# gMLP mixer of a streaming encoder: the rows of v by VectorE's 32x32 transposes and a DRAM scratch, in a lane of their own

## The chip, the cores and the metric

The kernel runs on one core of one Trainium2 chip. The metric is the device time of one execution in microseconds (us). The time before is 1324.58 us, the median of three runs (1324.56 to 1324.66).

## What is computed

One inference step of a two-layer encoder over 256 prompt frames and 32 sample frames, all in float32. The part that the change touches is the mixer of the odd layer:

```python
def _mixer_c(h, w_in, ln_g, ln_b, w_s, b_s, w_out):
    u, v = jnp.split(jax.nn.gelu(h @ w_in), 2, axis=-1)
    v = _layernorm(v, ln_g, ln_b)
    ...
    mixed = jnp.einsum('gij,bnjgc->bnigc', ws, vg) + b_s...
    return (u * mixed.reshape(B, T, D_C)) @ w_out, v
```

h has 1024 columns, u and v have 2048 each. The layer norm needs statistics over the 2048 columns of each frame. The einsum mixes frames (positions j to i) inside a window of 128 frames, in 8 groups of 256 columns.

## The kernel before

Activations lie transposed: columns on the 128 partitions, the 288 frames (32 of the sample, then 256 of the prompt) along the free axis. The six blocks of the network (`ffn`, `mixer_ab`, `ffn`, `ffn`, `mixer_c`, `ffn`) read their weights as one stream of chunks of up to 8 x 128 rows by 256 columns. SyncE (SP) fetches a chunk into one of three raw tiles `wraw` (`fetch`, L193). `pieces` then splits it in four pieces of 128x512: ScalarE (ACT) writes the rounded high part `wh` (L220), VectorE (DVE) subtracts for the low part `wl` (L221). A full chunk takes 48 products of 288 columns on TensorE (PE): for each of 8 row blocks and 2 column blocks the three products of `mm` (L260 to L262), the first of which reads `wl`. At the chunk's end `evac` (L309, DVE) takes the sums out of PSUM and multiplies them by the norm factor `rb`.

In the program's text, `next_chunk` finishes the splits of its own chunk, and `tick`, called after every 6 products, steps through the splits of the next one and through the lanes. A `Lane` is a list of generators that are worked off one after another, `rate` steps to a tick. This text order is not yet the engines' order: a scheduler places the instructions of every engine anew when the program is built, and each engine then works off its own list from front to back.

`mixer_c` takes 16 chunks of `c_w_in`: v in chunks v0 to v7 first, then u in u0 to u7, then the output projection (o0 and on), two chunks to each 256 output columns. After each v chunk ACT applies the Gelu: the sample's columns go to `vc` (L1005), the prompt's stay in `v` (L1007). The lane step `tokens` then turns v so that frames lie on the partitions: four TensorE transposes of 128x128 into one PSUM tile (L988), and an ACT copy to `vt` (L989); at odd n a fifth transpose for the sample (L994, L995) and `bn_stats` of both windows on DVE (L997). The same lane (`C_RATE` 0.5 steps a tick) holds `spatial_weights`, `row_sums`, and in the u chunks `statistics`, four `normed` (L1038 normalises `vt` and `vs` in place), `sample_out`, and `spatial(n)` for each u chunk: products of `vt` with the mixing weights (L1063, L1082) into the four PSUM tiles of the pool `misc`, DVE steps (L1086, L1089, L1094, L1095), and `put`, which casts u's part to `hh` (ACT, L329) and `hl` (DVE, L330) for the output projection. The u chunks' Gelu is L1102; their tile `u` has four buffers.

`to_rows` (L163), so far used in `mixer_ab` only, transposes a tile in 32x32 blocks on DVE (L168), writes it to a DRAM tile of the pool `rows` with four SP transfers (L172), and leaves it to the caller to read it back.

Of the kernel before, what the change touches and what calls it, by code (L numbers as in the profile page):

```python
# [14 lines left out]
P = 128  # L15
D = 1024
KD = D // P
TP = 256
TS = 32
# [12 lines left out]
WIN = ((32, 160), (160, 288), (0, 128))  # L32
# [40 lines left out]
class Lane:  # L73


    def __init__(self, rate):
        self.rate, self.credit, self.todo = rate, 0.0, []
# [16 lines left out]
class Net:  # L94
# [4 lines left out]
    def __init__(self, tc, ctx, I, O):  # L99
        self.tc, self.nc, self.I, self.O = tc, tc.nc, I, O  # L100
        e = ctx.enter_context
        self.const = e(tc.tile_pool(name="const", bufs=1))
        self.wraw = e(tc.tile_pool(name="wraw", bufs=3))
        self.wspl = e(tc.tile_pool(name="wspl", bufs=4))
        self.acc = e(tc.tile_pool(name="acc", bufs=2, space=PSUM))
        self.misc = e(tc.tile_pool(name="misc", bufs=4, space=PSUM))
        self.nrm = e(tc.tile_pool(name="nrm", bufs=1))
        self.rows = e(tc.tile_pool(name="rows", bufs=2, space=bass.MemoryType.DRAM))
        self.stream, self.pos = [], 0
        self.raw, self.spl = {}, {}  # L110
        self.uid = 0
        self.ahead = None
        self.lanes = []
        self.lv = None
        self.nlane = Lane(self.NORM_RATE)
# [805 lines left out]
    def mixer_c(self, gnext):  # L921
        nc, I, O = self.nc, self.I, self.O
# [3 lines left out]
        with self.tc.tile_pool(name="c", bufs=1, reuse_waits="tile") as pool:  # L926
            self.hidden(pool, 16)
            T = lambda tag, shape, bufs=None: self.t(pool, shape, tag, bufs=bufs)
            lane = Lane(self.C_RATE)
            self.lanes = [lane]  # L930


            J = N // 2
            vt, vs, vc = T("vt", [P, 2, DC]), T("vs", [P, J, P]), T("vc", [P, J, P])
            st = T("st", [P, 3, 4, 6])
# [30 lines left out]
            def row_sums():  # L966
                wsh, wsl = (self.t(pool, [P, 8, P + TS], n, F32R) for n in ("wsh", "wsl"))
                nc.scalar.copy(out=wsh, in_=wsT)
                yield
                nc.vector.tensor_tensor(out=wsl, in0=wsT, in1=wsh.bitcast(F32), op=ALU.subtract)  # L970
                for _ in range(4):
                    yield
                for a, e in ((0, 3), (3, 6), (6, 8)):
                    pt = self.ps("RS")
                    n = (e - a) * (P + TS)
                    mm(pt[:, :n], lhsT=self.onr, rhs=wsl[:, a:e], start=True, stop=False)
                    mm(pt[:, :n], lhsT=self.onr, rhs=wsh[:, a:e], start=False, stop=True)
                    nc.scalar.copy(out=rs[:, a:e], in_=pt[:, :n].rearrange("p (g i) -> p g i", i=P + TS))
                    yield

            def tokens(n, v):
                yield
                pv = self.ps("vt")
                for w in range(2):
                    for b in range(2):
                        s, e = WIN[w]
                        a = 256 * w + P * b
                        nc.tensor.transpose(pv[:, a:a + P], v[:, b, s:e], self.ident)  # L988
                nc.scalar.copy(out=vt[:, :, n * 256:n * 256 + 256], in_=pv.rearrange("p (w c) -> p w c", w=2))  # L989
                yield  # L990
                if n % 2:
                    j = n // 2
                    pv = self.ps("vs")
                    nc.tensor.transpose(pv[:, :P], vc[:, j], self.ident)  # L994
                    nc.scalar.copy(out=vs[:, j], in_=pv[:, :P])  # L995
                    for w in range(2):
                        nc.vector.bn_stats(st[:, w, j], vt[:, w, (n - 1) * 256:(n + 1) * 256])  # L997
                    yield

            spw = spatial_weights()  # L1000
            next(spw)
            for n in range(N):
                v = self.evac(pool, "v", 2)
                a = 2 * TS * (n % 2)
                nc.scalar.activation(out=vc[:, n // 2, a:a + 2 * TS].rearrange("p (b t) -> p b t", b=2),  # L1005
                                     in_=v[:, :, 0:TS], func=AF.Gelu_apprx_tanh)
                nc.scalar.activation(out=v[:, :, TS:], in_=v[:, :, TS:], func=AF.Gelu_apprx_tanh)  # L1007
                lane.todo.append(tokens(n, v))
                if n == 1:
                    lane.todo.append(spw)  # L1010
                if n == 3:
                    lane.todo.append(row_sums())
# [3 lines left out]

            def statistics():
                mv = state["mv"] = T("mv", [P, 3, 2])

                sp = T("sp", [P, 6])  # L1020
                nc.vector.bn_stats(sp, vs.rearrange("p j c -> p (j c)"))
                for k in range(4):
                    nc.vector.tensor_copy(out=st[0:TS, 2, k], in_=sp[TS * k:TS * k + TS])
                for w in range(3):
                    nc.vector.bn_aggr(mv[:, w], st[:, w])
                for k in range(1, 4):
                    nc.vector.tensor_copy(out=mv[TS * k:TS * k + TS, 2], in_=mv[0:TS, 2])
                ve = T("ve", [P, 3])
                nc.vector.tensor_scalar(out=ve, in0=mv[:, :, 1], scalar1=EPS, scalar2=None, op0=add)
                state["rs"] = self.power(ve, 3)  # L1030
                yield
# [9 lines left out]

            def sample_out():

                gb, bb, y = (T(n, [P, J, P]) for n in ("lng", "lnb", "vo"))
                for to, name in ((gb, "c_ln_g"), (bb, "c_ln_b")):
                    for k in range(4):
                        nc.gpsimd.dma_start(out=to[TS * k:TS * k + TS], in_=I[name][0].rearrange(
                            "(j k c) -> k j c", k=4, c=P)[k].partition_broadcast(TS))
                yield
                nc.vector.tensor_tensor(out=y, in0=vs, in1=gb, op=mul)  # L1050
                nc.vector.tensor_tensor(out=y, in0=y, in1=bb, op=add)
                for k in range(4):
                    nc.sync.dma_start(out=O[8][0, 0].rearrange("s (j k c) -> k s j c", k=4, c=P)[k],
                                      in_=y[TS * k:TS * k + TS])
                yield
# [44 lines left out]
            for n in range(N):  # L1100
                u = self.evac(pool, "u", self.C_LAG + 1)
                nc.scalar.activation(out=u, in_=u, func=AF.Gelu_apprx_tanh)  # L1102
                us[n] = u
                if n == 0:
                    lane.todo.append(statistics())
                    for s in range(4):
                        lane.todo.append(normed(s))
                    out = sample_out()
                    next(out)
                lane.todo.append(spatial(n))  # L1110
                if n == 0:
                    lane.todo.append(out)
# [269 lines left out]
```

## Time and profile before

| what | value |
|---|---|
| median of 3 runs | 1324.58 us |
| the profiled execution: its time, and its span | 1324.58 us, 1322.9 us |
| PE, PEld busy | 1317.1 us (100%), 1310.3 us (99%) |
| DVE, ACT, POOL busy | 887.1 us (67%), 661.7 us (50%), 41.7 us (3%) |
| the chain that ended last, by engine | PE 97%, DVE 2% |
| DMA, all queues | 219.83 MB, mean 166 GB/s |

PE is the matmul side of TensorE and PEld its weight loads, which overlap it. Matmuls are pipelined: a product's own record is longer than the distance to the next one's start. "Idle before" an instruction is the time its engine stood still ahead of it. The mixer of the odd layer lies between about 943 and 1118 us of the span; chunk v1's sums are taken at 954.38 us.

### The profile page before, as it was taken

How to read it: one execution, taken by the hardware profiler on the slowest of the kernel's cores; microseconds unless marked ns; L12 is line 12 of the kernel's file. 1: busy time of each engine (PE TensorE's matmuls, PEld its weight loads, DVE VectorE, ACT ScalarE, POOL GpSimd, SP SyncE). 2: the span in 40 equal slices, each digit the busy share in tenths (PEclk: the TensorE clock that was granted, in tenths of full speed). 3: DMA queues.
4: the chain of work that ended last, by engine and by line, in shares of the span. 5: the costliest groups of instructions: out<-in, count | busy, mean ns of one | idle time of the engine just before them, and what ended most of it. 6: DMA issues, size and time to landing. Idle time of an engine off the chain costs nothing.

```text
span 1322.9 us, 24562 instructions
## 1 busy us (share of the span) xinstructions
PE 1317.1 (100%) x9922; PEld 1310.3 (99%) x9922; DVE 887.1 (67%) x1706; ACT 661.7 (50%) x1355; POOL 41.7 (3%) x70
## 2 busy tenths in 40 slices
PE   9999999999999999999999999999999999999998
PEld 9999999999999999999999999999999999999998
DVE  7666556889898866666655756655567976666653
ACT  7544445464746465544444644444655446444432
POOL 1000000010101000000000000030000000000000
PEclk9999999999999999999999999999999999999999
DMA  9555455565565546555545555576544545555453
GB/s 283 178 176 168 150 175 173 157 182 159 168 170 170 140 134 200 161 178 166 157 153 174 165 179 165 161 183 188 169 152 138 167 147 160 173 166 171 152 152 84
DMA packets 254852, 219.83 MB, mean 166 GB/s; under 512 B 41233, under 2 KB 254018, under 8 KB 254738
## 3 DMA queue, kind: packets, MB, share of 16 engines
q1 hardware_dynamic: 253906, 216.32, 53.5%
q0 software_dynamic: 672, 1.77, 0.7%
q8 instruction: 78, 1.28, 0.4%
q10 hardware_dynamic: 160, 0.17, 0.1%
q14 instruction: 36, 0.29, 0.1%
HBM read 210.89 MB, written 7.34 MB: 165 GB/s over the span
## 4 chain that ended last, share of the span: by engine, by line
PE 97%; DVE 2%; ACT 0%; issue 0%; POOL 0%; DVEq 0%
PE acc L262 30%; PE acc L261 30%; PE acc L260 30%; PE sc L623 1%; DVE wl L221 1%; PE sp L1082 1%; PE S L696 0%; PE zs L833 0%; PE acc L1157 0%; PE sc L651 0%; PE ob L900 0%; PE vt L988 0%; PE acc L280 0%; PE z L845 0%; PE ob L895 0%
## 5 line engine op out<-in xcount | busy, mean ns | idle before, releaser
L220 ACT CAST wh<-wraw 128x512 fp32r<-128x512 f32 x768 | 440.5, 619 | 490.3 <-PE acc L262 370.1
L221 DVE TENSOR_TENSOR wl<-wraw,wh 128x512 fp32r<-128x512 f32 x768 | 507.4, 688 | 253.4 <-ACT wh L220 252.9
L260 PE MATMUL acc<-xh,wl 128*128 128x288 f32 x2096 | 627.2, 299 | 0.0
L261 PE MATMUL acc<-xl,wh 128*128 128x288 f32 x2096 | 619.4, 295 | 0.0
L262 PE MATMUL acc<-xh,wh 128*128 128x288 f32 x2096 | 618.9, 295 | 0.0
L261 PEld LDWEIGHTS acc<-xl,wh 128*128 128x128 f32 x2096 | 394.1, 188 | 0.6
L260 PEld LDWEIGHTS acc<-xh,wl 128*128 128x128 f32 x2096 | 393.9, 188 | 0.4
L262 PEld LDWEIGHTS acc<-xh,wh 128*128 128x128 f32 x2096 | 393.6, 188 | 0.2
L260 PE MATMUL acc<-hh,wl 128*128 128x288 f32 x960 | 284.5, 297 | 0.0
L261 PE MATMUL acc<-hl,wh 128*128 128x288 f32 x960 | 283.4, 295 | 0.0
L262 PE MATMUL acc<-hh,wh 128*128 128x288 f32 x960 | 282.8, 295 | 0.0
L260 PEld LDWEIGHTS acc<-hh,wl 128*128 128x128 f32 x960 | 180.2, 188 | 0.8 <-DVE xT L402 0.2
L261 PEld LDWEIGHTS acc<-hl,wh 128*128 128x128 f32 x960 | 180.3, 188 | 0.1
L262 PEld LDWEIGHTS acc<-hh,wh 128*128 128x128 f32 x960 | 180.3, 188 | 0.0
L309 DVE TENSOR_TENSOR u<-acc,rb 128x576 f32<-128x576 f32 x52 | 39.3, 757 | 48.8 <-PE acc L262 48.8
L309 DVE TENSOR_TENSOR g<-acc,rb 128x576 f32<-128x576 f32 x47 | 35.6, 757 | 47.0 <-PE acc L262 47.0
L329 ACT CAST hh<-u 128x576 fp32r<-128x576 f32 x52 | 35.1, 675 | 58.4 <-DVE u L455 40.3
L330 DVE TENSOR_TENSOR hl<-u,hh 128x576 fp32r<-128x576 f32 x52 | 39.4, 758 | 7.1 <-ACT hh L329 1.3
L336 ACT ACTIVATE xh<-xT,cols 128x288 fp32r<-128x288 f32 x40 | 21.2, 531 | 24.8 <-DVE xT L404 15.4
L455 DVE TENSOR_TENSOR u<-u,g 128x576 f32<-128x576 f32 x44 | 33.1, 752 | 0.0
L453 ACT ACTIVATE g<-g 128x576 f32<-128x576 f32 x44 | 30.0, 682 | 0.1
L404 DVE SCALAR_TENSOR_TENSOR xT<-acc,xT 128x288 f32<-128x288 f32 x32 | 14.5, 455 | 17.0 <-PE acc L262 17.0
(303 smaller groups left out, 759.1 us busy)
## 6 DMA issues: line engine op xcount, KB each, us to landing
wraw<-in_ffn_w_up_dram SPq DMA_DIRECT2D x44, 1024.0 KB, 5.9
wraw<-in_ffn_w_gate_dram SPq DMA_DIRECT2D x43, 1024.0 KB, 5.4
wraw<-in_ffn_w_down_dram SPq DMA_DIRECT2D x32, 1024.0 KB, 5.7
wraw<-in_ab_w_in_dram SPq DMA_DIRECT2D x28, 1024.0 KB, 5.0
wraw<-in_c_w_in_dram SPq DMA_DIRECT2D x16, 1024.0 KB, 5.5
wraw<-in_ffn_w_down_dram SPq DMA_DIRECT2D x16, 768.0 KB, 4.6
wraw<-in_c_w_out_dram SPq DMA_DIRECT2D x8, 1024.0 KB, 5.6
wraw<-in_ab_w_out_dram SPq DMA_DIRECT2D x8, 768.0 KB, 5.2
```

What stands on the lines that cost most here:

```text
L220: self.nc.scalar.copy(out=h[:, x], in_=w[:, a:b])
L221: self.nc.vector.tensor_tensor(out=l[:, x], in0=w[:, a:b], in1=h[:, x].bitcast(F32), op=ALU.subtract)
L260: mm(o, lhsT=l[:, k, c], rhs=hi[:, r], start=st, stop=False)
L261: mm(o, lhsT=h[:, k, c], rhs=lo[:, r], start=False, stop=False)
L262: mm(o, lhsT=h[:, k, c], rhs=hi[:, r], start=False, stop=en)
L309: self.nc.vector.tensor_tensor(out=x, in0=acc[:, :, :NT], in1=self.rb, op=ALU.mult)
L329: nc.scalar.copy(out=hh, in_=h)
L330: nc.vector.tensor_tensor(out=self.hl[:, k:k + 2], in0=h, in1=hh.bitcast(F32), op=ALU.subtract)
L336: nc.scalar.activation(out=self.xh[:, k], in_=x, func=AF.Copy, scale=g)
L404: nc.vector.scalar_tensor_tensor(out=x, in0=acc[b][:, :NT], scalar=scale, in1=x, op0=ALU.mult, op1=ALU.add)
L453: nc.scalar.activation(out=g, in_=g, func=AF.Silu)
L455: nc.vector.tensor_tensor(out=u, in0=u, in1=g, op=ALU.mult)
```

## The change

The rows of v no longer go through TensorE. `tokens` now makes two DVE transposes of 128x256 in 32x32 blocks (L168) into a tile named `lnb` or `vo` by turns, four SP writes to DRAM (L172), and two SP reads into `vt` (L989). These steps stand in a lane `fast` with one step a tick; all else stays in the lane with 0.5. The `bn_stats` of a pair of chunks move out into `means` (L982), which an even n calls for the pair before it, and `statistics` for the last pair. The DRAM pool has six buffers instead of two. The tiles `lng`, `lnb` and `vo` of `sample_out` get a flat shape of the same size. The fifth transpose, of the sample, stays.

```diff
--- before.py
+++ after.py
@@ -105,7 +105,7 @@
         self.acc = e(tc.tile_pool(name="acc", bufs=2, space=PSUM))
         self.misc = e(tc.tile_pool(name="misc", bufs=4, space=PSUM))
         self.nrm = e(tc.tile_pool(name="nrm", bufs=1))
-        self.rows = e(tc.tile_pool(name="rows", bufs=2, space=bass.MemoryType.DRAM))
+        self.rows = e(tc.tile_pool(name="rows", bufs=6, space=bass.MemoryType.DRAM))
         self.stream, self.pos = [], 0
         self.raw, self.spl = {}, {}
         self.uid = 0
@@ -926,8 +926,7 @@
         with self.tc.tile_pool(name="c", bufs=1, reuse_waits="tile") as pool:
             self.hidden(pool, 16)
             T = lambda tag, shape, bufs=None: self.t(pool, shape, tag, bufs=bufs)
-            lane = Lane(self.C_RATE)
-            self.lanes = [lane]
+            fast, lane = self.lanes = [Lane(1.0), Lane(self.C_RATE)]
 
 
             J = N // 2
@@ -978,24 +977,26 @@
                     nc.scalar.copy(out=rs[:, a:e], in_=pt[:, :n].rearrange("p (g i) -> p g i", i=P + TS))
                     yield
 
+            def means(j):
+                for w in range(2):
+                    nc.vector.bn_stats(st[:, w, j], vt[:, w, 512 * j:512 * j + 512])
+
             def tokens(n, v):
-                yield
-                pv = self.ps("vt")
-                for w in range(2):
-                    for b in range(2):
-                        s, e = WIN[w]
-                        a = 256 * w + P * b
-                        nc.tensor.transpose(pv[:, a:a + P], v[:, b, s:e], self.ident)
-                nc.scalar.copy(out=vt[:, :, n * 256:n * 256 + 256], in_=pv.rearrange("p (w c) -> p w c", w=2))
+                y = T(("lnb", "vo")[n % 2], [P, 2 * TP])
+                rows = self.to_rows(y, [(TP * b, v[:, b, TS:]) for b in range(2)])
+                for b in range(2):
+                    c = n * 256 + b * P
+                    nc.sync.dma_start(out=vt[:, :, c:c + P],
+                                      in_=rows[TP * b:TP * b + TP].rearrange("(w t) c -> t w c", t=P))
                 yield
                 if n % 2:
                     j = n // 2
                     pv = self.ps("vs")
                     nc.tensor.transpose(pv[:, :P], vc[:, j], self.ident)
                     nc.scalar.copy(out=vs[:, j], in_=pv[:, :P])
-                    for w in range(2):
-                        nc.vector.bn_stats(st[:, w, j], vt[:, w, (n - 1) * 256:(n + 1) * 256])
-                    yield
+                elif n:
+                    means(n // 2 - 1)
+                yield
 
             spw = spatial_weights()
             next(spw)
@@ -1005,7 +1006,7 @@
                 nc.scalar.activation(out=vc[:, n // 2, a:a + 2 * TS].rearrange("p (b t) -> p b t", b=2),
                                      in_=v[:, :, 0:TS], func=AF.Gelu_apprx_tanh)
                 nc.scalar.activation(out=v[:, :, TS:], in_=v[:, :, TS:], func=AF.Gelu_apprx_tanh)
-                lane.todo.append(tokens(n, v))
+                fast.todo.append(tokens(n, v))
                 if n == 1:
                     lane.todo.append(spw)
                 if n == 3:
@@ -1016,6 +1017,7 @@
 
             def statistics():
                 mv = state["mv"] = T("mv", [P, 3, 2])
+                means(J - 1)
 
                 sp = T("sp", [P, 6])
                 nc.vector.bn_stats(sp, vs.rearrange("p j c -> p (j c)"))
@@ -1041,7 +1043,7 @@
 
             def sample_out():
 
-                gb, bb, y = (T(n, [P, J, P]) for n in ("lng", "lnb", "vo"))
+                gb, bb, y = (T(n, [P, J * P]).rearrange("p (j c) -> p j c", c=P) for n in ("lng", "lnb", "vo"))
                 for to, name in ((gb, "c_ln_g"), (bb, "c_ln_b")):
                     for k in range(4):
                         nc.gpsimd.dma_start(out=to[TS * k:TS * k + TS], in_=I[name][0].rearrange(
```

How the change moves instructions. The number in a name counts the tiles of the program, so the same tile has another number in each version. The weights of chunks v7, u0, u1, u2 are `wraw_11212`, `11291`, `11367`, `11442` before, and `wraw_11230`, `11314`, `11405`, `11485` in the change; u3, u4, u5 are `11564`, `11654`, `11746` there.

DVE, from the last chunks of v to the first of u, before: sums of v6 (`v_11437`), v7 (`v_11514`) and u0 (`u_11598`) among the splits `wl`.

```order
L221 TENSOR_TENSOR wl_11485<-wraw_11291,wh_11484 128x512 x2
L221 TENSOR_TENSOR wl_11528<-wraw_11367,wh_11527 128x512 x2
L309 TENSOR_TENSOR v_11437<-acc_11366,rb_10949 128x576
L221 TENSOR_TENSOR wl_11569<-wraw_11367,wh_11568 128x512 x2
L309 TENSOR_TENSOR v_11514<-acc_11441,rb_10949 128x576
L997 BN_STATS st_10885<-vt_10882 128x6 x2
L221 TENSOR_TENSOR wl_11622<-wraw_11442,wh_11621 128x512 x2
L309 TENSOR_TENSOR u_11598<-acc_11518,rb_10949 128x576
```

The same place in the change: sums of v6 are `v_11480`, of v7 `v_11559`.

```order
L221 TENSOR_TENSOR wl_11457<-wraw_11230,wh_11456 128x512 x2
L309 TENSOR_TENSOR v_11480<-acc_11404,rb_10949 128x576
L168 STREAM_TRANSPOSE vo_11417<-v_11400 128x256 x2
L309 TENSOR_TENSOR v_11559<-acc_11484,rb_10949 128x576
L221 TENSOR_TENSOR wl_11494<-wraw_11314,wh_11493 128x512
L982 BN_STATS st_10885<-vt_10882 128x6 x2
L221 TENSOR_TENSOR wl_11494<-wraw_11314,wh_11493 128x512
L221 TENSOR_TENSOR wl_11536<-wraw_11314,wh_11535 128x512 x2
```

Before, the splits of u0 and u1 stand ahead of the taking of v7's sums. In the change the first split of u0 stands behind it.

ACT at the chunks u0 to u2, before: L1102 is the Gelu of u0 (`u_11598`) and u1 (`u_11703`), L220 casts the weights, here of u2 (`wraw_11442`), u3 (`11519`) and u4 (`11613`).

```order
L1102 ACTIVATE u_11598<-u_11598 128x576
L220 CAST wh_11657<-wraw_11442 128x512
L220 CAST wh_11715<-wraw_11519 128x512
L989 COPY vt_10882<-vt_11645 128x2x256
L220 CAST wh_11715<-wraw_11519 128x512
L995 COPY vs_10883<-vs_11667 128x128
L220 CAST wh_11750<-wraw_11519 128x512 x2
L1102 ACTIVATE u_11703<-u_11703 128x576
L220 CAST wh_11790<-wraw_11613 128x512 x2
```

In the change: L1104 is that Gelu, of u0 (`u_11639`), u1 (`u_11742`) and u2 (`u_11831`).

```order
L1104 ACTIVATE u_11639<-u_11639 128x576
L220 CAST wh_11572<-wraw_11405 128x512 x2
L220 CAST wh_11615<-wraw_11405 128x512 x2
L1104 ACTIVATE u_11742<-u_11742 128x576
L220 CAST wh_11662<-wraw_11485 128x512 x2
L220 CAST wh_11714<-wraw_11485 128x512 x2
L1104 ACTIVATE u_11831<-u_11831 128x576
```

Behind the Gelu of u0 there now stand the casts for u1, behind that of u1 those for u2; before, they were those for u2 and u3, and for u4.

DVE at the first `spatial`, in the change: the queue from the last `x` of `spatial(0)` to the first split of u5 (`wraw_11746`).

```order
L1091 SCALAR_TENSOR_TENSOR x_11804<-sp_11825,cols,z_11828 128x256
L1097 TENSOR_TENSOR u_11639<-xs_11783,u_11639 128x2x32
L1096 TENSOR_TENSOR u_11639<-x_11804,u_11639 128x2x256
L1052 TENSOR_TENSOR vo_11644<-vs_10883,lng_11642 128x512
L1088 SCALAR_TENSOR_TENSOR z_11897<-RS_10887,cols,BS_10888 128x128
L330 TENSOR_TENSOR hl_10881<-u_11639,hh_10880 128x576
L1053 TENSOR_TENSOR vo_11644<-vo_11644,lnb_11643 128x512
L1091 SCALAR_TENSOR_TENSOR x_11893<-sp_11894,cols,z_11897 128x256
L1088 SCALAR_TENSOR_TENSOR z_11917<-RS_10887,cols,BS_10888 128x128
L221 TENSOR_TENSOR wl_11933<-wraw_11746,wh_11932 128x512
```

Before, the same steps stand between splits, here of u4 (`wraw_11613`) and u5 (`wraw_11707`), one or two steps and then a split:

```order
L221 TENSOR_TENSOR wl_11836<-wraw_11613,wh_11835 128x512
L1074 TENSOR_TENSOR xs_11803<-xs_11803,zs_11802 128x128
L221 TENSOR_TENSOR wl_11836<-wraw_11613,wh_11835 128x512
L1089 SCALAR_TENSOR_TENSOR x_11822<-sp_11823,cols,z_11826 128x256
L1095 TENSOR_TENSOR u_11598<-xs_11803,u_11598 128x2x32
L221 TENSOR_TENSOR wl_11882<-wraw_11707,wh_11881 128x512
L1050 TENSOR_TENSOR vo_11603<-vs_10883,lng_11601 128x512
L221 TENSOR_TENSOR wl_11882<-wraw_11707,wh_11881 128x512
```

In the change nine `normed` steps (L1040) and twelve steps of `spatial` and `sample_out` follow each other without a split, after the four splits of u4. On PE they meet these products: the spatial products of groups 0 and 1 stand after 33 of the 48 products of chunk u4, where before they stood 12 products apart from chunk u3 on.

## Rows read from the trace of the kernel before

**Rows 1.** The page: the chain by engine; VectorE's splits, busy us, mean ns | idle before.

```profile
PE 97%; DVE 2%; ACT 0%; issue 0%; POOL 0%; DVEq 0%
...
L221 DVE TENSOR_TENSOR wl<-wraw,wh 128x512 fp32r<-128x512 f32 x768 | 507.4, 688 | 253.4 <-ACT wh L220 252.9
```

**Rows 2.** Windows: stretch, length; PE, PEld, DVE, ACT, POOL busy; PEclk, DMA share, GB/s.

```profile
945.00:1002.00 57.00, 56.98 (x432) 56.63 (x431) 37.31 (x66) 35.35 (x72) 0.00 (x0) 1.00 0.52 165
...
1019.00:1063.00 44.00, 44.00 (x345) 44.00 (x344) 42.71 (x97) 20.91 (x36) 0.00 (x0) 1.00 0.48 150
```

**Rows 3.** The chain, v chunks: start us, length us, what.

```profile
953.28 0.66 PE vt L988 x4
...
957.53 0.44 PE vt L988 x4
```

**Rows 4.** Tile vt: the transposes, duration ns min/median/max, first and last start.

```profile
L988 PE MATMUL vt<-ident,v x32: 270/272/328, 953.3 to 1006.4; 128*128 128x128 f32 x32
```

**Rows 5.** Timeline, PE and DVE at a chunk's end: start us, length us, what.

```profile
36.18 0.30 PE L262 MATMUL acc<-xh,wh 128*128 128x288 f32 x1
36.31 0.29 PE L260 MATMUL acc<-xh,wl 128*128 128x288 f32 x1
...
36.52 0.76 DVE L309 TENSOR_TENSOR u<-acc,rb 128x576 f32<-128x576 f32 x1 [1.20 <-PE acc L262]
```

**Rows 6.** Timeline, DVE and ACT from the sums of v6 to the next splits.

```profile
994.15 0.76 DVE L309 TENSOR_TENSOR v<-acc,rb 128x576 f32<-128x576 f32 x1
...
994.94 0.26 ACT L1005 ACTIVATE vc<-v 128x64 f32<-128x64 f32 x1 [0.20 <-DVE v L309]
...
995.80 1.14 ACT L220 CAST wh<-wraw 128x512 fp32r<-128x512 f32 x2
...
996.45 1.29 DVE L221 TENSOR_TENSOR wl<-wraw,wh 128x512 fp32r<-128x512 f32 x2 [1.55 <-ACT wh L220]
...
998.45 1.28 DVE L997 BATCH_NORM_STATS2 st<-vt 128x6 f32<-128x512 f32 x2
```

**Rows 7.** Timeline, ACT: a u chunk's Gelu and the casts behind it.

```profile
1027.00 0.69 ACT L1102 ACTIVATE u<-u 128x576 f32<-128x576 f32 x1
1027.59 1.12 ACT L220 CAST wh<-wraw 128x512 fp32r<-128x512 f32 x2
```

**Rows 8.** Groups of DVE by form, 940 to 1075 us: busy us, mean ns | idle before.

```profile
L1089 DVE SCALAR_TENSOR_TENSOR x<-sp,cols,z 128x256 f32<-128x256 f32 x16 | 7.6, 479 | 0.5 <-PE sp L1082 0.5
...
L330 DVE TENSOR_TENSOR hl<-u,hh 128x576 fp32r<-128x576 f32 x8 | 6.0, 753 | 1.3 <-ACT hh L329 1.3
L1086 DVE SCALAR_TENSOR_TENSOR z<-RS,cols,BS 128x128 f32<-128x128 f32 x16 | 5.5, 345 | 0.0
L1094 DVE TENSOR_TENSOR u<-x,u 128x512 f32<-128x512 f32 x8 | 5.5, 686 | 0.1
```

**Rows 9.** Timeline, DVE at the normalisation.

```profile
1013.54 0.16 DVE L1029 TENSOR_SCALAR ve<-mv 128x3 f32<-128x3 f32 x1
1014.70 1.00 DVE L1038 TENSOR_SCALAR vt<-vt,mv,pw 128x512 f32<-128x512 f32 x2 [1.00 <-POOL pw L134]
```

**Rows 10.** The chain at the mixer's end.

```profile
1070.32 0.40 PE acc L260
```

**Rows 11.** Line 168: DVE's 32x32 transposes, ns min/median/max.

```profile
L168 DVE STREAM_TRANSPOSE kn<-bv x4: 760/763/765, 268.1 to 451.6; 128x576 f32<-128x576 f32 x4
```

**Rows 12.** SP's timeline at a scratch write; DMA issues: KB each, us to landing.

```profile
242.91 2.05 SPq L172 DMA_DIRECT2D rows<-QK  x4
...
wraw<-in_c_w_in_dram SPq DMA_DIRECT2D x16, 1024.0 KB, 5.5
...
rows<-QK SPq DMA_DIRECT2D x16, 80.0 KB, 2.1
```

**Rows 13.** PE at the span's start (timeline), and spatial products in the chain.

```profile
1.16 3.36 PE L1157 MATMUL acc<-ones 128*128 128x128 f32 x14 [1.16 <-DVE ms L1168]
...
1060.79 1.78 PE sp L1082 x16
```

## The prediction, made before the result was known

> **What bounds the kernel now.** I read the page first: the chain of waits is 97% TensorE [rows 1]. The windows view says the same of the gMLP mixer: in the v chunks TensorE works 56.98 of 57 us, VectorE 37.3 and ScalarE 35.4; in the spatial part VectorE too is nearly full, 42.7 of 44 us [rows 2]. So a product taken from TensorE shortens the kernel by its distance to the next one, and anything that makes TensorE wait lengthens it by the wait. There is no slack in which a wait could vanish. What the reader is to see in the timeline is the reserve that keeps TensorE fed: VectorE stands idle for 1.20 us until the last product of a chunk has passed, takes the sums 0.34 us after that product's start, and TensorE's next product has long started, 0.13 us after it [rows 5]. It could, because the next chunk's weights were split beforehand.
>
> **What is removed.** 32 transposes. Each group of four fills 0.44 us of the chain, and the first one 0.66 because it waits for the Gelu [rows 3]: 7 x 0.44 + 0.66 = 3.7 us gained. A record of such a transpose lasts 272 ns [rows 4], but records overlap, and the distance of 0.11 counts. The Trainium skill, TensorE: Matmul & The Clock Gate, Part 4, gives about 275 ns for a transpose inside a kernel; the trace has that length too. By it the gain would be 32 x 0.275 = 8.8 us and the forecast below 5 us lower; the chain decides for 3.7. ScalarE loses eight copies, in idle time.
>
> **What is added.** 16 VectorE transposes of 256 columns. The nearest row has 763 ns for 576 columns [rows 11], so 0.34 us each by columns, 0.76 at most: 5 to 12 us in a stretch of 57 where VectorE idles for 20 [rows 2]. They cost nothing themselves. The DMAs: per chunk four writes, 2.05 us of SP's time, landing in about 2.1 us, and two reads, behind which the next weight fetch waits in SP's queue [rows 12]. A fetch lands in 5.5 us and is asked for more than a chunk (6.4 us) before its first split; in the new order the splits come later still, so I cost it at nothing. Without that cover a late fetch would cost its lateness.
>
> **What is moved is what counts.** The engines' orders show that the scheduler has laid VectorE's and ScalarE's queues anew. Before, the splits of u0 and u1 stand ahead of the taking of v7's sums. In the change the first split of u0 stands behind it, that of u1 behind u0's, and so on to u4. An engine works off its list from front to back, so VectorE idles through the chunk's products, and TensorE then waits for it. I add up each exposed chain, from the start of a chunk's last product; TensorE would otherwise go on after 0.13 us.
>
> Start of u0: 0.34 until VectorE takes v7's sums [rows 5], 0.67 until its next instruction starts (0.76 less 0.09, by which two splits of 0.69 that fill 1.29 overlap), 0.69 for the split [rows 1, 6], 0.03 for the hand-over to TensorE, taken as that from VectorE to ScalarE (994.15 + 0.76 to 994.94), less 0.13: 1.6 us.
>
> Starts of u1, u2, u3, u4: here ScalarE's queue has the Gelu of the chunk just ended ahead of the casts for the next, so the chain goes through both engines: 0.34, sums 0.76, hand-over 0.03, Gelu to cast 0.59 [rows 7], cast to split 0.65 [rows 6], split 0.69, hand-over 0.03, less 0.13 gives 2.96. The same chain stands in the trace once, hidden: from 994.15 to the end of the first split at 996.45 + 0.69 [rows 6] it takes 2.99, of which 0.16 are the extra Gelu on `vc`; with 0.34, 0.03 and 0.13 that makes 3.07. I take 3.03: four times, 12.1 us.
>
> Second splits: at u0, u2 and u4 a pair of `bn_stats` (1.2 us, [rows 6]) stands between the first and second split, 1.9 us from split to split where the first piece feeds 12 products, 1.6 us: 0.2 to 0.4 each, partly hidden at u0. 0.6 us.
>
> Spatial steps in u4: let T be the start of its first product. Two statistics, the aggregates and three splits bring `ve` to T+2.6; GpSimd's power and the way back take 1.16 [rows 9]; the nine `normed` steps, 0.46 apart, run from T+3.8 to T+8.0, the sample's (third) being done at T+5.25. TensorE wants it after 33 products, at T+4.8: 0.5 waited. The next waiting is for PSUM: the four `misc` tiles hold the first four spatial results, and the eighth group needs the fourth result read. That read is the eleventh step after `normed`: starts 0.2, 0.4, 0.2, 0.4, 0.14, 0.6, 0.6, 0.26, 0.67, 0.6 apart (the means less the overlap [rows 8], 0.6 also for the two steps on the output `vo`, 0.2 and 0.14 for the small ones), so it starts at T+12.0 and ends at T+12.5; TensorE gets there at T+10.0 (spatial pairs at 0.44 [rows 13]). 2.5 waited. The first split of u5 stands two places behind, done at T+13.35, and TensorE is ready at T+12.95: 0.4. Together 3.4 us.
>
> From u5 on VectorE's work for a chunk (4 splits, sums, one `spatial`) is about 6.3 us against 6.4 of products and 0.9 of spatial pairs, so the queue keeps pace. At the end of the mixer TensorE already lost a little before (0.40 instead of 0.13 [rows 10]). In the new order the first split of the second output chunk stands behind the last steps of `spatial(7)`, some 0 to 2.5 us of VectorE's work ahead of it [rows 8]; I take 1.3 us, the middle.
>
> **Sum:** -3.7 + 1.6 + 12.1 + 0.6 + 3.4 + 1.3 = +15.3 us. The profiled execution took 1324.58 us, the same as the median of the runs (its span is 1322.9), so I predict 1340 us. By the bounds (2.9 to 3.2 for each of the four chains, spatial 2 to 5, end 0 to 2.5) the likeliest case runs from 1336 to 1344.
>
> **Rivals.**
>
> 1. The clock falls. TensorE has never been idle this long in the trace, and its granted clock is 1.00 throughout [rows 2]; before its first work, products of 128 columns came 0.24 us apart against 0.11 later [rows 13], the ratio of 1.2 to 2.4 GHz, for about 4.5 us. If each of four waits of 3 us brought that back, each would cost 2.3 us more: 1349 us. For it: waits of 3 us in 9.4. Against it: two thirds of that time is dense work. 10%. The Trainium skill, TensorE: Matmul & The Clock Gate, Part 1, has the array fall back to 1.2 GHz after idling; no run here shows whether 3 us suffice.
>
> 2. The casts are not in the chain: if ScalarE had the next casts done before the Gelu, each of the four starts would cost 1.6 us as at u0, 5.7 less in all: 1334 us. The order speaks against it, since the Gelu stands ahead of the casts. 4%.
>
> 3. The rows of v land late, and `bn_stats` waits for the scratch. From transposes to landed reads I bound it by 0.8 + 2.05 + 2.1 + 0.75 + 5.5, some 11 us [rows 12]; the last pair's statistics stand three chunks behind its transposes, over 20 us. If a read were 4 us over that, TensorE would wait: 1344 us. 3%.
>
> 4. Faster: the gain stays alone. That needs TensorE to have the next chunk's first split at hand at each of the five starts, as it has today [rows 5], so that less than 3.7 us are waited in all; the point from which it decides is one and a quarter exposed chains. 1324.6 - 3.7 = 1320.9 us. The only way is that the queues as executed let a split pass a waiting instruction; the idle 1.20 us on VectorE ahead of each taking of sums [rows 5] speaks against it. 3%.
>
> 5. Only one chain is exposed, for a reason that I don't see: 3.7 lost, 3.7 gained, no change. 2%.
>
> **How the numbers follow.** The likeliest case has what remains, 78%. About 0.2%, 2.7 us, is what a measurement of this kernel tells from no change. Faster by more: rival 4, 0.03. Within: rival 5, 0.02. Slower: all others, 0.95. The range from 1335 to 1346 holds the likeliest case, rival 3 and part of a falling clock (one to three of the four waits), and leaves out a good tenth.
>
> **What would show it.** In the changed kernel's profile TensorE's busy share stays high by its modelled records, but its weight loads should show idle times of about 1.6 us once and 3 us four times, released by `wl` L221, one behind each of the chunks v7, u0, u1, u2 and u3, then 0.5, 2.5 and 0.4 us around the first spatial products; VectorE should idle 4 to 5 us ahead of its L309 there, and ScalarE's Gelu L1104 be followed at once by casts, each followed by a split and TensorE's start. The stretch between the sums of v7 and of u3 should take four times 9.4 us instead of 6.4. The prediction is wrong if TensorE runs through these starts, if a wait for `vt` or for `wraw` from DMA stands ahead of a split, or if the granted clock leaves 1.00.

## The result and the profile after

The changed kernel takes 1347.69 us (median of 4 runs, 1346.91 to 1348.67) against 1324.57 for the kernel before: ratio 1.0175, 95% interval 1.0157 to 1.0192. It is slower, as forecast, but 7.7 us beyond the forecast of 1340 and outside its range of 1335 to 1346. The profiled execution took 1348.28 us, 23.7 more than that of before, with a span of 1346.6 us.

The page, beside [rows 1]: the chain by engine, then two groups (busy us, mean ns | idle before).

```profile
PE 91%; DVE 4%; issue 3%; ACT 1%; POOL 0%; POOLq 0%; DVEq 0%; ACTq 0%
...
L260 PE MATMUL acc<-xh,wl 128*128 128x288 f32 x2096 | 631.0, 301 | 13.3 <-DVE wl L221 13.1
...
L260 PEld LDWEIGHTS acc<-xh,wl 128*128 128x128 f32 x2096 | 397.9, 190 | 14.9 <-issue 14.1
```

TensorE's share of the chain falls from 97 to 91%, and 13.3 us of idle time, 13.1 of them ended by VectorE's split, stand ahead of the first product of a chunk. The windows (columns as in [rows 2]): first the v chunks, then one from each start of u0 to u4 to the next, the last of these up to the wait of the spatial products, then the spatial part:

```profile
945.00:1002.00 57.00, 54.77 (x407) 53.93 (x406) 38.51 (x82) 28.25 (x60) 0.00 (x0) 1.00 0.71 185
993.10:1001.40 8.30, 6.76 (x52) 6.54 (x51) 7.11 (x18) 1.04 (x3) 0.00 (x0) 1.00 0.43 137
1001.40:1012.40 11.00, 8.11 (x50) 7.90 (x50) 3.94 (x7) 2.75 (x5) 2.17 (x4) 0.84 0.96 217
1012.40:1024.60 12.20, 9.31 (x50) 9.10 (x50) 4.44 (x7) 2.75 (x5) 0.00 (x0) 0.72 0.53 170
1024.60:1035.60 11.00, 8.11 (x50) 7.91 (x50) 3.25 (x5) 2.75 (x5) 0.00 (x0) 0.84 0.31 97
1035.60:1049.20 13.60, 10.71 (x74) 10.51 (x73) 11.13 (x26) 6.23 (x12) 1.25 (x1) 0.87 0.24 77
1049.20:1060.20 11.00, 8.99 (x56) 8.57 (x55) 11.00 (x27) 3.96 (x7) 0.00 (x0) 0.84 0.30 78
```

The column before the last two tells what the sum of waits missed: a chunk takes 11.0, 12.2 and 11.0 us instead of the forecast 9.4, and the granted clock in it is 0.72 to 0.84, where it was 1.00 in the stretches of before [rows 2]. One start, that of u2, in the timeline of VectorE and ScalarE:

```profile
1012.83 0.76 DVE L309 TENSOR_TENSOR u<-acc,rb 128x576 f32<-128x576 f32 x1 [5.81 <-PE acc L262]
1013.62 0.68 ACT L1104 ACTIVATE u<-u 128x576 f32<-128x576 f32 x1 [8.25 <-DVE u L309]
1014.21 2.16 ACT L220 CAST wh<-wraw 128x512 fp32r<-128x512 f32 x4
1014.84 0.69 DVE L221 TENSOR_TENSOR wl<-wraw,wh 128x512 fp32r<-128x512 f32 x1 [1.26 <-ACT wh L220]
1015.45 1.28 DVE L982 BATCH_NORM_STATS2 st<-vt 128x6 f32<-128x512 f32 x2
```

and in that of TensorE's weight loads, of which there is one to each product:

```profile
1012.23 0.19 PEld L261 LDWEIGHTS acc<-xl,wh 128*128 128x128 f32 x1
1012.37 0.19 PEld L262 LDWEIGHTS acc<-xh,wh 128*128 128x128 f32 x1
1015.65 0.29 PEld L260 LDWEIGHTS acc<-xh,wl 128*128 128x128 f32 x1 [3.10 <-issue]
1015.82 0.33 PEld L261 LDWEIGHTS acc<-xl,wh 128*128 128x128 f32 x1
1016.06 0.33 PEld L262 LDWEIGHTS acc<-xh,wh 128*128 128x128 f32 x1
```

Here is the forecast chain: sums, Gelu, cast, split, TensorE, 3.28 us from the last product of u1 to the first of u2, and VectorE idle for 5.81 us ahead of the sums. Behind it products start 0.24 us apart instead of 0.13, which is 1.2 instead of 2.4 GHz; 25 of them in this chunk, 13, 15 and 13 behind the starts of u1, u3 and u4, and 14 from 1052.5 on, behind the wait of the spatial products. At 0.107 us more each, the 80 products cost 8.5 us.

The waits add up from the same column of starts. Over all distances above 0.26 us in the mixer, less 0.13 for each, the trace gives 19.86 us, that of before 0.73. So: 19.1 of waits, 8.5 of half clock, less 32 x 0.11 = 3.5 for the transposes: 24.1, where the profiled executions differ by 23.7. I use this account for every run below.

### The profile page after: what moved, and what is told of

Same layout as the page of the kernel before. It is cut to its first block, busy times and chain, and to the rows that moved or that the text cites. A ratio compares the mean times of both kernels' runs of the same rounds, so it can differ in the third digit from the quotient of the medians.

```text
span 1346.6 us, 24619 instructions
## 1 busy us (share of the span) xinstructions
PE 1323.6 (98%) x9890; PEld 1315.0 (98%) x9890; DVE 891.0 (66%) x1722; ACT 656.8 (49%) x1347; POOL 41.9 (3%) x70
## 4 chain that ended last, share of the span: by engine, by line
PE 91%; DVE 4%; issue 3%; ACT 1%; POOL 0%; POOLq 0%; DVEq 0%; ACTq 0%
PE acc L262 28%; PE acc L261 28%; PE acc L260 28%; DVE wl L221 1%; PE sc L623 1%; PE S L696 0%; PE zs L833 0%; ACT wh L220 0%; DVE x L1091 0%; PE acc L1159 0%; PE sc L651 0%; PE ob L900 0%; DVE vt L1040 0%; PE acc L280 0%; PE z L845 0%
## 5 line engine op out<-in xcount | busy, mean ns | idle before, releaser
L220 ACT CAST wh<-wraw 128x512 fp32r<-128x512 f32 x768 | 439.1, 618 | 487.5 <-PE acc L262 367.4
L260 PE MATMUL acc<-xh,wl 128*128 128x288 f32 x2096 | 631.0, 301 | 13.3 <-DVE wl L221 13.1
L260 PEld LDWEIGHTS acc<-xh,wl 128*128 128x128 f32 x2096 | 397.9, 190 | 14.9 <-issue 14.1
L337 DVE SCALAR_TENSOR_TENSOR xl<-xT,cols,xh 128x288 fp32r<-128x288 f32 x40 | 20.6, 514 | 8.5 <-ACT xh L336 8.5
```

What stands on the lines that cost most here:

```text
L220: self.nc.scalar.copy(out=h[:, x], in_=w[:, a:b])
L260: mm(o, lhsT=l[:, k, c], rhs=hi[:, r], start=st, stop=False)
L337: nc.vector.scalar_tensor_tensor(out=self.xl[:, k], in0=x, scalar=g, in1=self.xh[:, k].bitcast(F32), op0=ALU.mult, op1=ALU.subtract)
```

## The experiments

Two questions: what lays the splits behind the sums, and whether the clock's 8.5 us come from TensorE's idleness. "Half-clock products" are those that start 0.24 us behind the one before instead of 0.13, or, for the shorter spatial products and transposes, 0.21 instead of 0.11.

**e1. The writes on GpSimd.**

```diff
-            nc.sync.dma_start(out=to[q], in_=y[TS * q:...
+            (q_ or nc.sync).dma_start(out=to[q], in_=y[TS * q:...
...
-                rows = self.to_rows(y, [...])
+                rows = self.to_rows(y, [...], nc.gpsimd)
```

> The changed kernel with the four scratch writes of a chunk issued by GpSimd; the two reads stay on SP, and nothing else is edited. Theory (the loss comes from where the scheduler puts the splits, and it puts them late because of the writes in SP's queue): in the new order the first split of u0 to u4 stands 5 to 9 places ahead of the taking of the sums of the chunk before, so TensorE does not wait there; the 32 transposes stay gone, the granted clock stays at 1.00: 1324.6 - 3.7 = 1321 us (1319 to 1323). Rival A (the transposes on VectorE and the trip through DRAM cost the time themselves, wherever they are issued): four waits of about 3 us remain at the starts of u1 to u4, 1337 to 1348 us. Rival B (GpSimd's issuing is slow and the rows land late): a wait for vt ahead of bn_stats, 1323 to 1335 us.

Measured: 1326.45 us (11 runs, 1324.10 to 1328.18), ratio 1.0012 [1.0003, 1.0021]. VectorE's order, around the sums of v7 (line, operation, out<-in):

```
L221 TENSOR_TENSOR wl_11573<-wraw_11405,wh_11572 128x512 x2
L309 TENSOR_TENSOR v_11559<-acc_11484,rb_10949 128x576
L221 TENSOR_TENSOR wl_11616<-wraw_11405,wh_11615 128x512 x2
```

These are splits of u1; all four of u0 stand ahead of them again, and 21 of the 23 us are gone with one edit that leaves every transpose on VectorE and every byte of the trip. Rival A falls. The waits at the starts of u0 to u4 are gone altogether; what remains is rival B, at another place. The timeline, VectorE and TensorE's weight loads:

```profile
1016.77 1.29 DVE L982 BATCH_NORM_STATS2 st<-vt 128x6 f32<-128x512 f32 x2 [1.32 <-DMA vt<-rows]
...
1018.30 0.19 PEld L260 LDWEIGHTS acc<-xh,wl 128*128 128x128 f32 x1
1021.12 0.50 PEld L1065 LDWEIGHTS sp<-wsB,vs 128*128 128x128 f32 x2 [2.63 <-issue]
```

The last statistics wait 1.3 us for rows from DRAM, the normalised `vs` is late by so much, and the first spatial product waits 2.7 us; 15 half-clock products follow. So the rows explain half of this wait; the rest is left to the 4.4 us from these statistics to that product. A transpose of `vc` adds 0.8. The runs part by the clock as well: those with a mean of 1.000 took 1324.1 to 1325.3, those with 0.997 1328.0 and 1328.2.

**e2. The order by hand.**

```diff
+            with self.tc.manual_schedule(engines={mybir.EngineType.DVE}):
                 for n in range(N):
                     v = self.evac(pool, "v", 2)
                     ...
```

> The changed kernel with VectorE's instructions of the v chunks kept in the order in which the program writes them; all scratch transfers stay on SP. Theory (the order alone makes the loss): the first splits of u0 to u4 stand 5 to 24 places ahead of the sums, no waits at these starts, clock 1.00: 1321 us (1318 to 1324). Rival (SP is really too slow: with six transfers a chunk in its queue the weights of the next chunk land late, and the scheduler's late places only mirror that): TensorE waits at the starts of u1 to u4 all the same, now for a split that waits for wraw from DMA: 1335 to 1348 us.

Measured: 1329.26 us (5 runs), ratio 1.0039 [1.0026, 1.0051]. Neither was right. With all six transfers of a chunk still on SP the starts of u1 to u4 do not wait, so SP's queue does not make those waits on the chip. But in the program's order VectorE comes to `bn_stats` before the rows are there (timeline in chunk u0; the last two rows show what stands behind it):

```profile
999.00 1.29 DVE L982 BATCH_NORM_STATS2 st<-vt 128x6 f32<-128x512 f32 x2 [4.53 <-DMA vt<-rows]
1000.21 1.88 DVE L221 TENSOR_TENSOR wl<-wraw,wh 128x512 fp32r<-128x512 f32 x3
1000.93 0.19 PEld L260 LDWEIGHTS acc<-xh,wl 128*128 128x128 f32 x1 [1.45 <-DVE wl L221]
```

Three such waits, 9.4 us on VectorE, come through to TensorE as 1.2 to 1.5 us behind the first twelve products of v4, v6 and u0, where the second split is wanted, and the transposes of `vc` in these chunks then wait 1.1 each. The profiled run has no half-clock products; two of the other four show a mean clock of 0.997 and 0.998.

**e3 and e9. Work in the waits.** The dummy products write columns 384 to 511 of a PSUM tile, which nothing reads. As the scheduler places them, the trace of e3 has 8 ahead of u0 and 12 ahead of each of u1 to u4. In e9 the last three counts are 9 instead of 12.

```diff
+        for _ in range(self.fill):
+            self.nc.tensor.matmul(acc[0][:, 384:512], lhsT=self.ones, rhs=self.ones, start=True, stop=True)
         self.mm(acc, ch, (self.xh, self.xl), self.KORD, True, True)
...
+                self.fill = (7, 12, 1, 12, 12, 12, 0, 0)[n]
                 u = self.evac(pool, "u", self.C_LAG + 1)
```

> The changed kernel with dummy products added (ones by ones, into columns of the next chunk's PSUM tile that nobody reads), 8 ahead of u0 and 12 ahead of each of u1 to u4; they sit in TensorE's queue where it waits. VectorE's order is that of the changed kernel. Theory (the 7.7 us beyond the sum of the waits come from the granted clock, which falls because TensorE stands idle in each wait): the distance from the last product of a chunk to the first of the next stays near 3.2 us, the clock stays at 1.00 and the time falls by 6 to 8 us, to 1340 us (1339 to 1342), though work is added. Rival (the clock falls for another reason, or the 7.7 us lie elsewhere): 1346 to 1350 us with a clock below 1.00 as in the changed kernel.

> As e3 with 9 instead of 12 dummy products ahead of u2, u3 and u4. In e3 the dummies at these starts began only 1.27 us after the chunk's last product (they wait for the PSUM tile until VectorE has taken the sums) and 12 of 0.22 us then ran 0.66 past the end of the wait, so that the start took 3.94 us instead of 3.28. Theory: starts of 3.3 us again, the clock still at 1.00 behind them, 3 x 0.66 less than e3: 1340.7 us (1339.5 to 1341.7), 7 us under the changed kernel though it waits as long. Rival (the clock in e3 stayed up because the distances were other ones, not because TensorE worked in them): half clock again behind these starts, 1344 us or more.

Measured: e3 1342.67 us (4 runs), ratio 1.0141 [1.0127, 1.0155]; e9 1342.30 us (4 runs), ratio 1.0134 [1.0119, 1.0150]. Windows of e9, from start to start as above:

```profile
1001.50:1010.90 9.40, 9.28 (x74) 9.09 (x73) 3.94 (x7) 2.75 (x5) 2.17 (x4) 1.00 0.96 221
1010.90:1020.60 9.70, 8.85 (x69) 8.51 (x68) 4.44 (x7) 2.75 (x5) 0.00 (x0) 1.00 0.73 208
1020.60:1030.10 9.50, 8.65 (x68) 8.41 (x68) 3.26 (x5) 2.76 (x5) 0.00 (x0) 1.00 0.46 151
```

VectorE and ScalarE do what they did in the changed kernel, a chunk's first product still starts 3.2 to 3.3 us after the last of the chunk before, and the clock stays at 1.00: 9.4, 9.7 and 9.5 us where it was 11.0, 12.2 and 11.0. That is the prediction's 9.4. So the clock fell there because TensorE stood idle; adding work made the kernel 5.4 us faster. Both runs missed their figure, by 2.7 and 1.6 us. In e3 twelve dummies were too many, and three starts took 3.94 us. In both, TensorE, no longer slowed, is early at the spatial products: in e9 it waits 0.9 us ahead of the first, where the changed kernel has no wait, and again 2.5 at a later one, with 12 half-clock products behind it in the profiled run; two of the four runs show a mean clock of 1.000.

**e4. The trip beside the transposes.** Nobody reads the rows here.

```diff
                 nc.scalar.copy(out=vt[:, :, n * 256:...     (TensorE's transposes stay)
+                y = T(("lnb", "vo")[n % 2], [P, 2 * TP])
+                rows = self.to_rows(y, [...])
+                for b in range(2):
+                    nc.sync.dma_start(out=z[:, :, P * b:P * b + P], in_=rows[...])
```

> The kernel before with tokens(n, v) in the lane of its own and with the scratch trip added beside the TensorE transposes: VectorE transposes each chunk into y, SP writes it to DRAM and reads it back into a tile that nobody uses; vt still comes from TensorE, and bn_stats stand where they stood before. Theory (SP's transfers in the scheduler's plan push the splits behind the sums; neither the removal of the transposes nor the lane does): the first splits of u1 to u4 stand 1, 9, 8 and 6 places behind the sums, TensorE waits 3 us or more at each, the clock falls with it: 1338 to 1352 us, over the 1324.6 of before. Rival (the loss belongs to what the change takes from TensorE or to bn_stats waiting for the rows): within 3 us of 1324.6.

Measured: 1337.05 us (4 runs), ratio 1.0097 [1.0082, 1.0113]. TensorE loses nothing of its work, the statistics wait for no row, and the kernel is 12.5 us slower, of which e5 puts 1.6 down to the lane: the trip alone lays the order anew, and by e1 it is its writes in SP's queue that do it. The time is 1 us under the range, and the theory had the waits too long: TensorE stands 4.0 us at the start of u1, but 1.4 at that of u2 and 0.1 and 0.8 at u3 and u4, with 1.1 and 2.0 ahead of spatial products, and half-clock products follow at u1 alone. The longest of the waits, at the start of u1:

```profile
1004.48 0.19 PEld L262 LDWEIGHTS acc<-xh,wh 128*128 128x128 f32 x1
...
1006.21 1.00 DVE L1043 TENSOR_SCALAR vt<-vt,mv,pw 128x512 f32<-128x512 f32 x2 [1.00 <-POOL pw L134]
1007.12 0.75 DVE L309 TENSOR_TENSOR u<-acc,rb 128x576 f32<-128x576 f32 x1
1007.79 1.88 DVE L221 TENSOR_TENSOR wl<-wraw,wh 128x512 fp32r<-128x512 f32 x3
...
1008.58 0.19 PEld L260 LDWEIGHTS acc<-xh,wl 128*128 128x128 f32 x1 [3.91 <-issue]
```

**e5. The lane alone.**

```diff
-            lane = Lane(self.C_RATE)
-            self.lanes = [lane]
+            fast, lane = self.lanes = [Lane(1.0), Lane(self.C_RATE)]
...
-                lane.todo.append(tokens(n, v))
+                fast.todo.append(tokens(n, v))
```

> The kernel before with tokens(n, v) in the lane of its own and nothing else of the change: TensorE's transposes stay, no trip through DRAM, bn_stats where they stood. Theory (the lane does no harm): every first split stands 4 places or more ahead of the sums, no new waits, 1324.5 us (1323.5 to 1326). Rival (steps that run right behind the Gelu make TensorE wait for v, or push the splits back): 1327 us or more, with waits of PEld ahead of the transposes into vt.

Measured: 1326.15 us (10 runs), ratio 1.0013 [1.0003, 1.0022], between the two figures. The order is harmless, as the theory has it, but the rival's wait is there: TensorE's transposes now stand 0.2 to 0.8 us for the Gelu, eight times, 2.5 us in all (one of them, 0.3, is in before too). The lane is worth little either way.

**e6, e7, e8, e10. Some chunks by rows, the rest by TensorE.** With `HYB` = 6, 4, 6 and 7; e8 keeps all transfers on SP and the old place of the transposes of `vc`.

```diff
+                if n >= HYB:
+                    ...                     (the transposes of before)
                 y = T(("lnb", "vo")[n % 2], [P, 2 * TP])
-                rows = self.to_rows(y, [...])
+                rows = self.to_rows(y, [...], nc.gpsimd)
...
                 if n % 2:
+                    yield
                     j = n // 2
```

> Writes issued by GpSimd as in e1, but only the chunks v0 to v5 go by way of the scratch; v6 and v7 keep TensorE's transposes, so that the statistics no longer wait for the last rows; and the transposes of vc come one step later. Theory (what e1 still lost was the wait of 2.8 us ahead of the first spatial product, the half clock behind it, and the 0.9 us ahead of a transpose of vc): 24 transposes gone, 24 x 0.11 = 2.7 us less than before, none of these waits: 1321.8 us (1321 to 1323.5). Rival (rows from DRAM cost something that no wait shows): 1324 to 1326 us.

> As e6 with v0 to v3 by way of the scratch and v4 to v7 by TensorE's transposes. Theory: 16 transposes gone, 1.8 us less than before: 1322.7 us (1321.8 to 1324), about 0.9 us over e6. Rival: no order between e6, e7 and before.

> The changed kernel with v0 to v5 by way of the scratch, all transfers on SP, and v6 and v7 by TensorE's transposes. In its order the first splits of u0, u1 and u2 stand 2, 1 and 1 places behind the sums, those of u3 on 9 and more ahead. Theory (each exposed start costs its wait and, where it is as long as the four of the changed kernel, about 1.5 us of half clock): -2.7 + 1.8 at u0 + 2 x 3.15 + 2 x 1.5 + 0.5 for a transpose of vc = about +9: 1333.5 us (1330 to 1337). Rival A (SP's six transfers a chunk delay the weights themselves): waits at u3 and u4 too, 1337 us or more. Rival B (the clock needs four waits in a row to fall): 1330 us, clock 1.00.

> As e6 with v0 to v6 by way of the scratch and v7 alone by TensorE's transposes: 28 transposes gone. Theory: 28 x 0.11 = 3.1 us less than before, 1321.6 us (1320.8 to 1323), if the rows of v6, now the last to land, are there when the statistics want them. Rival: they are not, a wait ahead of the first spatial product as in e1, 1323 us or more.

Measured: e6 1322.10 us (11 runs), ratio 0.9983 [0.9974, 0.9992]; e7 1323.27 (11 runs), 0.9993 [0.9985, 1.0002]; e8 1334.47 (4 runs), 1.0074 [1.0060, 1.0088]; e10 1327.47 (8 runs), 1.0025 [1.0015, 1.0036].

e6 is faster than both kernels, by 2.4 us of the 2.7 forecast; e7 lies 1.2 over it, not told from before by its interval, in the order forecast. In e6 TensorE's windows are full again, beside [rows 2]:

```profile
945.00:1002.00 57.00, 57.00 (x428) 56.46 (x427) 43.22 (x88) 34.20 (x71) 19.78 (x32) 1.00 0.82 231
1019.00:1063.00 44.00, 44.00 (x343) 43.89 (x341) 41.51 (x93) 21.28 (x37) 0.00 (x0) 1.00 0.49 150
```

e8 puts the same rows back on SP and loses 12 us: u0, u1 and u2 are exposed, as its order says, and u3 and u4 are not. Windows of e8, one that holds the start of u0, one from the start of u1 to that of u2, one with the start of u2:

```profile
994.30:1005.70 11.40, 8.95 (x56) 8.53 (x55) 7.61 (x18) 3.71 (x8) 0.00 (x0) 0.85 0.53 172
1005.70:1013.90 8.20, 6.66 (x51) 6.45 (x50) 3.16 (x5) 0.68 (x1) 0.00 (x0) 1.00 0.39 125
1013.90:1024.00 10.10, 6.75 (x37) 6.05 (x36) 7.67 (x17) 5.97 (x11) 1.25 (x1) 0.83 0.25 76
```

Rivals A and B both fall: two of three waits, at u0 and u2, brought half clock, and in e1 and e10 one wait alone does. The split of the loss was other than forecast: 2.9 at u0 (a transpose of v7 for its Gelu, then the split), 1.8 at u1, 3.15 at u2, 1.0 ahead of a spatial product.

e10 comes out as its rival has it, by other rows. One chunk more by rows, and the statistics ask for rows that are not there (timeline: VectorE, SP, TensorE's weight loads):

```profile
983.13 0.77 DVE L168 STREAM_TRANSPOSE vo<-v 128x256 f32<-128x256 f32 x2
...
995.86 3.50 SPq L1008 DMA_DIRECT2D vt<-rows  x4
...
1005.90 1.29 DVE L982 BATCH_NORM_STATS2 st<-vt 128x6 f32<-128x512 f32 x2 [4.11 <-DMA vt<-rows]
...
1014.68 0.50 PEld L1085 LDWEIGHTS sp<-wsB,vs 128*128 128x128 f32 x2 [4.47 <-issue]
```

The transposes shown are those of v5: the semaphores that these statistics wait for are those that tell of the landing of v4's and v5's reads, not of v6's, whose statistics at 1008.90 do not wait for DMA. From v5's transposes to the statistics 22.8 us pass. Its reads, the first two of the four shown, are issued behind a weight fetch in SP's queue and have landed at 1005.78; in e6 the same reads have landed at 1001.95. Whether v6's reads, issued just behind them, made the difference is not shown. TensorE then stands 4.5 us ahead of the first spatial product, and 22 half-clock products follow.

**The account.** Microseconds against before, from the profiled executions; waits as above, less before's 0.7 (in e3 and e9 they include the dummies):

| run | waits | half clock | transposes gone | sum | measured |
|---|---|---|---|---|---|
| changed | 19.1 | 80: 8.5 | -3.5 | 24.1 | 23.7 |
| e1 | 3.9 | 15: 1.6 | -3.5 | 2.0 | 1.9 |
| e2 | 8.2 | 0 | -3.5 | 4.7 | 4.4 |
| e3 | 21.9 | 11: 1.2 | -3.5 | 19.6 | 19.5 |
| e4 | 11.7 | 14: 1.5 | 0 | 13.2 | 12.4 |
| e5 | 2.3 | 0 | 0 | 2.3 | 1.3 |
| e6 | 0.3 | 0 | -2.6 | -2.3 | -2.5 |
| e7 | 0.8 | 0 | -1.8 | -1.0 | -1.4 |
| e8 | 10.0 | 23: 2.5 | -2.6 | 9.9 | 10.0 |
| e9 | 20.7 | 12: 1.3 | -3.5 | 18.5 | 18.1 |
| e10 | 4.6 | 22: 2.4 | -3.1 | 3.9 | 3.8 |

Every run closes within 1.0 us, without a fourth term.

## Why the prediction missed

**What bounds the kernel: right.** To 0.4 us, the result is waits and slower products of TensorE, less the transposes.

**What is removed: right.** 0.11 us per transpose holds; e7 to e6, eight transposes more, are 1.2 us, and e6's 24 are 2.4. The transposes' records of 0.27 us, by which 24 would give 6.5, are ruled out.

**What is added: right in the changed kernel.** VectorE's transposes last 0.42 us (inside the bounds of 0.34 and 0.76) and lie in its idle time; the weight fetches land in 5.9 instead of 5.5 us, and no split there waits for one:

```profile
wraw<-in_c_w_in_dram SPq DMA_DIRECT2D x16, 1024.0 KB, 5.9
...
L168 DVE STREAM_TRANSPOSE lnb<-v x8: 398/418/446, 952.7 to 1000.4; 128x256 f32<-128x256 f32 x8
```

**What is moved: right in place, and nearly in price.** Waits of 19.1 us where the terms gave 19.0; that they agree to 0.1 is partly luck, since terms that came out smaller or not at all make up for chains that are 0.1 to 0.2 us longer and for a wait that was not foreseen:

| step | forecast | measured |
|---|---|---|
| start of u0 | 1.6 | 1.8 |
| starts of u1 to u4 | 4 x 3.03 | 4 x 3.15 |
| second splits | 0.6 | 0, in none of the distances |
| spatial steps in u4 | 0.5 + 2.5 + 0.4 | 0 + 2.15 + 0.4 |
| end of the mixer | 1.3 | 1.7 more than before |
| a transpose of `vc` ahead of its Gelu | none | 0.8 |

The 0.5 was hidden, since TensorE at half clock came later to it, and so were the second splits of u2 and u4: in e9, at full clock, the first is 0.9, the others 0.2 and 0.3. At u0 the second split waits in neither. The prediction put the moved splits down to the scheduler; e1, e4 and e8 add the reason, SP's transfers in the scheduler's plan. Why its plan sends splits back for them is not seen in a trace and stays open.

**The step that failed is the clock.** The sum prices every product behind a wait at full pace, that is, the falling clock at nothing; only rival 1 has it, with a chance of 10%, held down by "two thirds of that time is dense work", and the range had room for one to three such falls. The fall came on top of the likeliest case, behind all four waits of 3.28 us and a fifth time behind the spatial wait: 80 products at half clock, 8.5 us, and e3 and e9 show that those behind the starts go away when TensorE works in the waits. The Trainium skill, TensorE: Matmul & The Clock Gate, Part 1, says that the array falls back to 1.2 GHz after idling; the prediction noted that no run showed whether 3 us suffice. Here they did, at all four starts, and so the question bore on the price of the likeliest case, not on a side case. That the rival's 1349 us is only 1.3 over the result is partly luck: it had 2.3 us behind each of four waits, from the slow products at the span's start, and the runs show 1.4, 2.7, 1.6 and 1.4, with 1.5 at the fifth place, which it did not name. (In the trace of before, the slow products at the span's start follow each other in 0.21 us, not 0.24, and go on until 6.4 us, not 4.5.) Take the 8.5 us off the profiled 1348.28, and 1339.8 is left, where 1340 was forecast. That too is partly luck: e9 shows that a kernel with these waits and a full clock takes 1342, since part of what the half clock takes had covered other waits.

**Rival 3 did not occur, but depends on the order.** In the changed kernel no `bn_stats` waits. The prediction bounded the trip by some 11 us; in e2, with all transfers on SP as there, the statistics that wait for rows start 10.7, 12.0 and 10.8 us after the transposes, close to it. With the writes on GpSimd it is longer: 18.9 us for the last rows of e1, 22.8 in e10. The late order that costs TensorE its splits is also what hides the rows' lateness. Rivals 2, 4 and 5 did not occur.

## What to carry to other kernels

Price a new wait of a bound TensorE twice: its length, and the products behind it at half clock, 1.1 to 2.7 us for each wait of about 3 us here. Ask of a new transfer not only how long it takes but what its queue does to the order in which a scheduler lays the other engines' work: the same change costs 23 us with its writes on SP and 2 with them on GpSimd. And take a slow route only as far as its results are asked for late: six of eight chunks by rows gained 2.4 us; seven lost 3, to a wait for rows.

## What the runs showed of the hardware that was not expected

- Distances from one product's start to the next across a wait of TensorE (0.13 us more than the wait), and what followed in the profiled runs: 3.28 us, four times, 13 to 25 half-clock products; 3.29 (e8), 10; 4.1 and 4.66 (e4, e10), 14 and 22; 2.82 (e1), 15; 2.29 (changed), 14; 2.62 (e3, e9), 11 and 12; in e8 2.14 and 1.04 one behind the other, 13. Behind 1.94 (changed, e8), 1.3 to 1.7 (e2) and 2.15 (e4) there are none. It differs from run to run: in e3 and e9 the profiled runs have a mean clock of 0.998, while five of the eight runs of both show 1.000; in e2 the profiled run shows 1.000, two others 0.997 and 0.998.
- The fall need not come with the first products behind a wait. It does at u1, u2 and u4 of the changed kernel; at u3 the first six go at full pace (from 1027.84, half from 1028.66), and in e8, behind the wait of 3.29 us, TensorE has been back for about 2 us (full pace from 1017.13, half from 1018.97).
- A dummy product of 128 by 128 fp32 fills 0.22 us of TensorE, and with nine to twelve of them in each wait the clock stayed at 1.00 over four starts (e3, e9).
